# Attention scores of two heads in the two halves of the array's rows, in three passes of 64 rows

## The chip, the cores and the metric

The kernel runs on one core of one Trainium2 chip. The metric is the device time of one execution in microseconds; three runs of the kernel before took 1248.9, 1249.17 and 1249.78 us, median 1249.17. The core has a matrix engine (PE, with the loading of its weights shown apart as PEld), a vector engine (DVE), a scalar engine (ACT), a third elementwise engine (POOL) and SP, whose queue issues nearly all transfers.

## What is computed

Two layers over 512 tokens of width 1024, all in float32: an attention with a forget gate in the first, a gated short convolution in the second, each followed by an MLP with a squared ReLU and a gated embedding, with RMSNorm around everything. The change touches the attention alone, 16 heads of 64:

```python
proj = h @ w_in
q, k, v = ...                        # per head, HEAD_DIM = 64
q = q * HEAD_DIM ** -0.5
c = cumsum(log_sigmoid(f_logit))     # per head, along the tokens
s = einsum('bhqd,bhkd->bhqk', qb, k) # 128 queries at a time
s = s + cb[..., :, None] - c[..., None, :]
s = where(k_pos <= q_pos, s, NEG_INF)
pr = softmax(s)
o = einsum('bhqk,bhkd->bhqd', pr, v)
return o @ w_out
```

## The kernel before

**Numbers in two parts.** Matrix operands are kept as a pair of tiles, hi (the value rounded to the type that PE streams) and lo (the rest). `split` (L219) makes them: a copy on ACT (L221) gives hi, a subtraction on DVE (L222) gives lo. A product takes three matmuls, `mm3` (L211): hi times hi (L213), and the two mixed ones (L214, L215); the product of the two lo parts is left out. Tiles are pages of 128 x 512 from one pool of 70; matmuls write into eight PSUM banks of the same shape.

**One list for PE.** From L611 on a loop over steps `c` deals out the attention's work, and PE runs it in the order that the scheduler makes of it. `stream` (L548) supplies the filling work: `project(i)` for pair after pair of heads (48 matmuls of 512 columns each: k first, then q), then parts of the output projection (`out_part`). `share` (L614) says how many units of it are due by step `c`: two a step until the seven projections that are left are out, then 18 output units over the remaining steps. A step also has:

- `turn(h, j)` (L484): for head `h` and a block `j` of 128 keys, up to four transposes (L487) of the weights into a bank `pT`, split into `ph` and `pl`. Where columns have to be filled with zeros, POOL does it (L494).
- `mix(h, j)` (L498), two steps later (`LAG`): the values times `ph` and `pl` (L509, L510) into `ps_o`; after the last block ACT and DVE add the two halves of its rows (L514, L515).
- `scores(h, b)` (L463), eight steps ahead of the transposes: for head `h` and its block `b` of 128 queries, two matmuls (L471, L472) over `max(128 * (b + 1), 256)` key columns. Then a reduction with the bias on DVE (L474), the exponential on ACT (L478), a reciprocal on DVE (L479) and the normalisation on POOL (L480).
- `bias(h)` (L445), one head ahead of the scores (`LEAD`): four loads of the cumulated gate from DRAM on SP's queue (L457) and four masks on POOL (L458), into the tiles that the scores then become.

**How a head's score takes two matmuls.** `project(i)` brings the q of two heads into one bank, head 0 in rows 0 to 63, head 1 in rows 64 to 127, and k the same. Per head (L430 to L442) it makes three pages. `qs` holds the hi part of the head's q in the head's own 64 rows (L434, ACT) and its lo part in the other 64 rows (L435, DVE). `kh` and `kl` hold the split of k in the head's own rows, and two transfers on SP's queue (L442) copy each into the other 64 rows. A matmul over all 128 rows then adds up q-hi and q-lo times the same part of k, so that two of them, with `kh` and with `kl`, give all four products.

The last two steps' matmuls are put in order by hand (`BY_HAND`). After the loop the rest of the output projection follows (`mixer_out`, L317), and the MLP.

Of the kernel before, what the change touches and what calls it, by code (L numbers as in the profile page):

```python
# [8 lines left out]
F32 = mybir.dt.float32  # L9
F32R = mybir.dt.float32r  # L10
AF = mybir.ActivationFunctionType
ALU = mybir.AluOpType
# [3 lines left out]
P = 128  # L16
D = 1024
S = 512
H = 16
HD = 64  # L20
# [6 lines left out]
LAG = 2  # L27
# [3 lines left out]
LEAD = 1  # L31
# [4 lines left out]
BLOCKS = ((0, 0), (1, 0), (0, 1), (1, 1), (2, 1), (3, 1), (2, 0), (3, 0))  # L36
EARLY = 4
BY_HAND = 2
LEFT = 10
LATE = 0  # L40

# [21 lines left out]
def trunk(ctx: ExitStack, tc, x, pT, g, wv, wqk, bf, wo, wci, cw, wco, wup, wdn, wpp, wpg, out):  # L63
    nc = tc.nc
# [9 lines left out]
    def page(name, dtype=F32):  # L74
        return pages.tile([P, S], dtype, tag="pg", name=name)

    def bank(name):
        return psum.tile([P, S], F32, tag="ps", name=name)

    def stat(name, n=1, dtype=F32):  # L80
        return small.tile([P, n], dtype, tag=f"st{n}", name=name, bufs=32 if n == 1 else 8)
# [72 lines left out]
    def narrow(*key, k, c, soon=SOON):  # L154

        c += k % 2 * 256
        return wide(*key, k // 2, soon=soon).at(lambda u: u[:, c : c + P])
# [53 lines left out]
    def mm3(ps, a, b, start, stop):  # L211

        nc.tensor.matmul(ps, a.hi, b.hi, start=start, stop=False)  # L213
        nc.tensor.matmul(ps, a.lo, b.hi, start=False, stop=False)  # L214
        nc.tensor.matmul(ps, a.hi, b.lo, start=False, stop=stop)  # L215
        streamed[0] += 3 * ps.shape[-1]
        due()

    def split(hi, lo, src, eng=nc.vector):  # L219

        nc.scalar.copy(hi, src)  # L221
        eng.tensor_tensor(out=lo, in0=src, in1=hi.bitcast(F32), op=ALU.subtract)  # L222
# [24 lines left out]
    def stats(t, xs, name):  # L247
        return rstd([squares(xs[n][:, :S], f"{name}_q{n}_{t}") for n in range(2)], f"{name}_r{t}")
# [86 lines left out]
    def attention(hT, first_x, g0, by_hand):  # L335
# [79 lines left out]
        stacked, probs, outs, both = {}, {}, {}, {}  # L415

        def project(i):

            heads = [[page(f"{n}{i}_{e}", F32R) for n in ("qs", "kh", "kl")] for e in range(2)]
            stacked[i] = heads  # L420
            for s in (1, 0):
                ps = bank(f"qk{i}_{s}")
                for k in range(KT):
                    mm3(
                        ps, narrow("qk", i, k=k, c=s * P),
                        hT.at(lambda h: h[:, k, :]), k == 0, k == KT - 1,
                    )
                    if k < KT - 1:
                        yield
                for e in range(2):  # L430
                    a, b = slice(64 * e, 64 * e + 64), slice(64 - 64 * e, 128 - 64 * e)
                    q, kh, kl = heads[e]
                    if s == 0:
                        nc.scalar.mul(q[a, :S], ps[a, :], HD**-0.5)  # L434
                        nc.vector.scalar_tensor_tensor(  # L435
                            out=q[b, :S], in0=ps[a, :], scalar=HD**-0.5,
                            in1=q[a, :S].bitcast(F32), op0=ALU.mult, op1=ALU.subtract,
                        )
                    else:
                        split(kh[a, :S], kl[a, :S], ps[a, :])  # L440
                        for h in (kh, kl):
                            nc.sync.dma_start(h[b, :S].bitcast(F32), h[a, :S].bitcast(F32))  # L442
                yield

        def bias(h):  # L445


            i, e = h // 2, h % 2
            if e == 0:
                both[i] = page(f"pr{i}")  # L450
            long, rest = page(f"prl{h}"), page(f"prr{h}")
            probs[h] = [
                rest[:, 384:512], both[i][:, 256 * e : 256 * e + 256], rest[:, :384], long[:, :S],
            ]
            for b, pr in enumerate(probs[h]):
                n = (b + 1) * P
                nc.sync.dma_start(pr, neg_c[b, h : h + 1, :n].partition_broadcast(P))  # L457
                nc.gpsimd.affine_select(  # L458
                    out=pr[:, b * P : n], in_=pr[:, b * P : n], compare_op=ALU.is_ge,
                    fill=NEG, base=0, pattern=[[-1, P]], channel_multiplier=1,  # L460
                )

        def scores(h, b):  # L463

            q, kh, kl = stacked[h // 2][h % 2]
            n = (b + 1) * P
            nm = max(n, 256)
            pr = probs[h][b]
            ps = bank(f"sc{h}_{b}")
            qb = q[:, b * P : n]  # L470
            nc.tensor.matmul(ps[:, :nm], qb, kh[:, :nm], start=True, stop=False)  # L471
            nc.tensor.matmul(ps[:, :nm], qb, kl[:, :nm], start=False, stop=True)  # L472
            nmx, sm, rs = (stat(f"{s}{h}_{b}") for s in ("nmx", "sm", "rs"))
            nc.vector.tensor_tensor_reduce(  # L474
                out=pr, in0=ps[:, :n], in1=pr, scale=-1.0, scalar=3e38, op0=ALU.add,
                op1=ALU.min, accum_out=nmx,
            )
            nc.scalar.activation(pr, pr, AF.Exp, bias=nmx, scale=-1.0, accum_out=sm)  # L478
            nc.vector.reciprocal(rs, sm)  # L479
            nc.gpsimd.tensor_scalar(out=pr, in0=pr, scalar1=rs, scalar2=None, op0=ALU.mult)  # L480

        weights, mixed = {}, {}

        def turn(h, j):  # L484
            ps = bank(f"pT{h}_{j}")
            for b in range(j, NB):
                nc.tensor.transpose(  # L487
                    ps[:, b * P : (b + 1) * P], probs[h][b][:, j * P : (j + 1) * P], ident
                )
            lo_q = min(j * P, S - 256)  # L490
            ph, pl = page(f"ph{h}_{j}", F32R), page(f"pl{h}_{j}", F32R)
            if lo_q < j * P:
                for z in (ph, pl):
                    nc.gpsimd.memset(z[:, lo_q : j * P].bitcast(F32), 0.0)  # L494
            split(ph[:, j * P : S], pl[:, j * P : S], ps[:, j * P :])
            weights[h, j] = (ph, pl)

        def mix(h, j):  # L498

            e = h % 2  # L500
            if j == 0:
                mixed[h] = bank(f"ps_o{h}")
                if e == 0:
                    outs[h // 2] = page(f"oT{h // 2}")
            ps_o = mixed[h]
            lo_q = min(j * P, S - 256)
            v = vs[j][h // 4][:, h % 4 * P : (h % 4 + 1) * P]
            ph, pl = weights.pop((h, j))
            nc.tensor.matmul(ps_o[:, lo_q:], v, ph[:, lo_q:S], start=j == 0, stop=False)  # L509
            nc.tensor.matmul(ps_o[:, lo_q:], v, pl[:, lo_q:S], start=False, stop=j == NB - 1)  # L510
            if j == NB - 1:
                a, b = slice(64 * e, 64 * e + 64), slice(64 - 64 * e, 128 - 64 * e)
                o2 = page(f"o2{h}")
                nc.scalar.copy(o2[a, :S], ps_o[b, :])  # L514
                nc.vector.tensor_tensor(  # L515
                    out=outs[h // 2][a, :S], in0=ps_o[a, :], in1=o2[a, :S], op=ALU.add
                )
                if e == 1:
                    complete.append(h // 2)
                    split_o()  # L520
# [27 lines left out]
        def stream():  # L548
            for i in range(1, KT):
                yield from project(i)  # L550
            yield from out_part((0,), range(6))
            yield from out_part((1,), range(6))
            prepare(where["o", 1, KT - 1] + 1)
            yield from out_part((0, 1), (6,))
# [13 lines left out]
        with tc.manual_schedule(engines={E.PE, E.DVE, E.Activation}):  # L568
            r = stats(0, first_x[0], name)
# [22 lines left out]
            out=ones[:, :S], in_=ones[:, :S], compare_op=ALU.is_ge, fill=0.0, base=0,  # L592
# [15 lines left out]
        for _ in range(8):  # L608
            next(main)
        n_sc, done = 4 * H, 8  # L610
        for c in range(-8, n_sc + LAG):  # L611
            if c == n_sc - BY_HAND:
                by_hand.enter_context(tc.manual_schedule(engines={E.PE}))
            share = 2 * (c + 9) if c < n_sc - 16 else 112 + (c - n_sc + 17) * (28 - LEFT) // (15 + LAG)  # L614
            while done < share + AHEAD:
                next(main, None)
                done += 1
            if 0 <= c < n_sc:
                turn(c // 4, c % 4)
            if c >= LAG:  # L620
                mix((c - LAG) // 4, (c - LAG) % 4)
            if c + 8 < n_sc:
                scores((c + 8) // 4, c % 4)
            if c % 4 == 0 and 1 < (c + 8) // 4 + LEAD < H:
                bias((c + 8) // 4 + LEAD)
        for _ in main:
            pass
        return oT[0], banks_o
# [226 lines left out]
    hT = turned_x  # L855
    by_hand = ExitStack()
    lhs, opened = attention(hT, first_x, g0, by_hand)
    oT = lhs
    lhs = lambda k, t: tokens(oT, k, t)
# [97 lines left out]
```

## Time and profile before

| what | value |
|---|---|
| the profiled execution's own time | 1248.93 us |
| its span, first to last instruction | 1247.2 us |
| mean granted clock of PE | 0.998 |
| matmuls of the scores (L471, L472) | 64 + 64, from 81.2 to 216.9 us |
| transposes (L487) | 160, from 92.1 us on |
| mixes (L509, L510) | 64 + 64, from 96.4 to 231.1 us |
| copies of kh and kl (L442) | 16 + 16, 128 KB each |

The profile is of one execution. Times in it are microseconds unless marked ns. A matmul's row gives the line, the tile it writes, the tiles it reads, the rows and columns of the weights (128\*128) and the rows and columns of what streams (128x512). Matmuls overlap in a pipeline and their ends are modelled, so that a row's duration is longer than the distance to the next start. A wait row reads: who waited, for whom, us in total, times, longest.

### The profile page before, as it was taken

The page shows a single profiled execution, that of the slowest core. Times are in us where ns is not written, and L with a number is a line of the kernel's source. Part 1 is how long each engine was busy: PE and PEld are TensorE (multiplying, and loading weights), DVE is VectorE, ACT ScalarE, POOL GpSimd, SP SyncE. Part 2 cuts the span into 40 slices and gives each one's busy share as a digit, 9 for nine tenths or more (in the row PEclk, how much of TensorE's full clock was granted, in tenths as well). Part 3 has the DMA queues.
Part 4 walks back from the last instruction along what each step waited for, and adds up shares of the span by engine and source line. Part 5 has one row for each costly group of instructions (what it writes and reads, how often), then busy time and mean ns, then how long its engine had stood idle before and what let it go on. Part 6 is the DMA issues. An engine that isn't in the chain of part 4 may idle for free.

```text
span 1247.2 us, 18012 instructions
## 1 busy us (share of the span) xinstructions
PE 1221.6 (98%) x5972; PEld 1023.2 (82%) x5972; DVE 918.0 (74%) x1402; ACT 612.6 (49%) x1309; POOL 633.9 (51%) x631
## 2 busy tenths in 40 slices
PE   7999999999999999999999999999999999999997
PEld 6888887887888888888789888889788888888876
DVE  5657878676789778989877444457778898779972
ACT  5456777546544543454555223333654345535451
POOL 2016667256878777775211000017777778778210
PEclk9999999999999999999999999999999999999999
DMA  7456564532343224428224232432422442236401
GB/s 256 147 159 166 152 157 115 186 116 78 100 135 110 80 82 135 136 74 277 76 83 133 68 100 90 148 119 69 131 63 78 135 135 94 67 110 190 148 18 51
DMA packets 85789, 148.68 MB, mean 119 GB/s; under 512 B 10112, under 2 KB 17328, under 8 KB 85696
## 3 DMA queue, kind: packets, MB, share of 16 engines
q1 hardware_dynamic: 85488, 147.27, 38.2%
q8 instruction: 47, 0.77, 0.3%
q14 instruction: 46, 0.38, 0.1%
q10 hardware_dynamic: 144, 0.26, 0.1%
q0 software_dynamic: 64, 0.00, 0.0%
HBM read 136.93 MB, written 6.37 MB: 115 GB/s over the span
## 4 chain that ended last, share of the span: by engine, by line
PE 69%; DVE 13%; POOL 5%; issue 5%; ACT 4%; DMA 3%; SPq 0%; DVEq 0%; POOLq 0%; ACTq 0%
DVE wl L222 6%; PE up L214 6%; PE up L215 6%; PE up L213 6%; PE dn L214 5%; PE dn L213 5%; PE dn L215 5%; PE pg L213 2%; PE pg L214 2%; PE pg L215 2%; PE qk L214 2%; PE qk L213 2%; PE qk L215 2%; POOL s L715 2%; ACT junk L244 2%
## 5 line engine op out<-in xcount | busy, mean ns | idle before, releaser
L222 DVE TENSOR_TENSOR wl<-raw,wh 128x512 fp32r<-128x512 f32 (+1 forms) x404 | 364.7, 953 | 25.3 <-ACT wh L221 24.3
L221 ACT CAST wh<-raw 128x512 fp32r<-128x512 f32 (+1 forms) x404 | 219.7, 619 | 9.5 <-DVE xd L295 5.0
L214 PE MATMUL up<-hTh,wl 128*128 128x512 f32 (+1 forms) x576 | 210.1, 365 | 0.0
L215 PE MATMUL up<-hTl,wh 128*128 128x512 f32 (+1 forms) x576 | 209.8, 366 | 0.0
L213 PE MATMUL up<-hTh,wh 128*128 128x512 f32 (+1 forms) x576 | 209.3, 366 | 0.0
L222 POOL TENSOR_TENSOR wl<-T,wh 128x512 fp32r<-128x512 f32 x112 | 161.0, 1469 | 35.7 <-ACT wh L221 32.0
L213 PEld LDWEIGHTS up<-hTh,wh 128*128 128x128 f32 x576 | 108.6, 189 | 17.7
L214 PEld LDWEIGHTS up<-hTh,wl 128*128 128x128 f32 x576 | 108.6, 189 | 17.6
L215 PEld LDWEIGHTS up<-hTl,wh 128*128 128x128 f32 x576 | 108.3, 189 | 17.5 <-DVE hTl L222 0.2
L747 DVE TENSOR_TENSOR acc<-dn,acc 128x512 f32<-128x512 f32 x168 | 107.3, 679 | 8.5 <-PE dn L215 8.5
L130 POOL TENSOR_TENSOR T<-raw,raw 128x512 f32<-128x512 f32 x56 | 87.8, 1579 | 36.2 <-DMA raw<-in_wdn 23.7
L701 ACT ACTIVATE r<-up 128x512 f32<-128x512 f32 (+1 forms) x72 | 38.7, 546 | 122.7 <-PE up L215 114.7
L130 POOL TENSOR_TENSOR T<-raw,T 128x512 f32<-128x512 f32 x56 | 90.9, 1623 | 2.2
L687 DVE TENSOR_TENSOR q<-r 128x512 f32<-128x512 f32 (+1 forms) x72 | 68.6, 959 | 28.8 <-ACT r L701 28.6
L236 POOL TENSOR_SCALAR cor_r_v<-cos,cos 128x1 f32<-128x1 f32 x4 | 1.6, 398 | 159.1 <-ACT junk L244 159.1
L221 ACT CAST A11h<-q 128x256 fp32r<-128x256 f32 x28 | 11.4, 407 | 102.0 <-DVE q L687 102.0
L221 ACT CAST wh<-T 128x512 fp32r<-128x512 f32 x112 | 61.2, 617 | 0.0
L213 PE MATMUL pg<-wh,hTh 128*128 128x512 f32 x128 | 50.9, 397 | 3.5 <-ACT hTh L221 3.3
L754 POOL TENSOR_TENSOR acc<-acc,acc 128x512 f32<-128x512 f32 x28 | 46.9, 1706 | 10.1 <-DVE acc L747 10.1
L213 PE MATMUL qk<-hTh,wh 128*128 128x512 f32 x128 | 51.1, 399 | 0.0
L215 PE MATMUL qk<-hTl,wh 128*128 128x512 f32 x128 | 50.9, 397 | 0.0
L214 PE MATMUL pg<-wh,hTl 128*128 128x512 f32 x128 | 50.3, 393 | 0.0
(234 smaller groups left out, 3082.5 us busy)
## 6 DMA issues: line engine op xcount, KB each, us to landing
raw<-in_wup SPq DMA_DIRECT2D x128, 256.0 KB, 2.9
raw<-in_wdn SPq DMA_DIRECT2D x128, 256.0 KB, 2.9
raw<-in_wci SPq DMA_DIRECT2D x48, 256.0 KB, 3.2
raw<-in_wqk SPq DMA_DIRECT2D x32, 256.0 KB, 3.4
raw<-in_wpg SPq DMA_DIRECT2D x32, 256.0 KB, 3.5
g<-in_g SPq DMA_DIRECT2D x22, 256.0 KB, 5.9
prl<-neg_c SPq DMA_DIRECT2D x16, 256.0 KB, 6.6
raw<-in_wo SPq DMA_DIRECT2D x16, 256.0 KB, 5.1
```

The costliest lines, as they stand in the source:

```text
L130: nc.gpsimd.tensor_tensor(out=B[name, p], in0=B[a, p], in1=B[b, p], op=ALU.subtract)
L213: nc.tensor.matmul(ps, a.hi, b.hi, start=start, stop=False)
L214: nc.tensor.matmul(ps, a.lo, b.hi, start=False, stop=False)
L215: nc.tensor.matmul(ps, a.hi, b.lo, start=False, stop=stop)
L221: nc.scalar.copy(hi, src)
L222: eng.tensor_tensor(out=lo, in0=src, in1=hi.bitcast(F32), op=ALU.subtract)
L244: nc.scalar.activation(junk, src, AF.Square, scale=D**-0.5, accum_out=ss)
L687: nc.vector.tensor_tensor(out=out, in0=r, in1=r, op=ALU.mult)
L701: nc.scalar.activation(r[:, :n], ps[:, :n], AF.Relu)
L715: sums = lambda out, a, b, op: nc.gpsimd.tensor_tensor(out=out, in0=a, in1=b, op=op)
L747: nc.vector.tensor_tensor(out=a, in0=banks[s], in1=a, op=ALU.add)
L754: nc.gpsimd.tensor_tensor(out=a, in0=a, in1=acc[i, s][:, :S], op=ALU.add)
```

## The change

The pages of a pair are now four: `qh`, `ql`, `kh`, `kl`, each with head 0 in rows 0 to 63 and head 1 in rows 64 to 127, as the bank has them. Each is made by one instruction over 128 rows; there is no copy between rows. `scores(i, b)` takes a pair of heads: three products for each head (hi hi, hi lo, lo hi, without lo lo), each a matmul over the head's 64 rows, written in turns for head 0 and head 1 into two banks. The vector work after it is as before, head after head.

The loop is fitted to pairs: scores are issued at every second step, 12 steps ahead of the transposes instead of 8 (`SCORED`), so that the loop starts at -12; the projections run out at step 43 instead of 47, and the 18 output units are spread over the steps from 44 on; the bias of a pair's even head is issued 7 steps before its scores, that of the odd head 4 steps before.

```diff
+SCORED = 12
...
-            heads = [[page(f"{n}{i}_{e}", F32R) for n in ("qs", "kh", "kl")] for e in range(2)]
-            stacked[i] = heads
+            q, key = (Pair(page(f"{n}h{i}", F32R), page(f"{n}l{i}", F32R)) for n in "qk")
+            stacked[i] = q, key
...
-                for e in range(2):
-                    a, b = slice(64 * e, 64 * e + 64), slice(64 - 64 * e, 128 - 64 * e)
-                    q, kh, kl = heads[e]
-                    if s == 0:
-                        nc.scalar.mul(q[a, :S], ps[a, :], HD**-0.5)
-                        nc.vector.scalar_tensor_tensor(
-                            out=q[b, :S], in0=ps[a, :], scalar=HD**-0.5,
-                            in1=q[a, :S].bitcast(F32), op0=ALU.mult, op1=ALU.subtract,
-                        )
-                    else:
-                        split(kh[a, :S], kl[a, :S], ps[a, :])
-                        for h in (kh, kl):
-                            nc.sync.dma_start(h[b, :S].bitcast(F32), h[a, :S].bitcast(F32))
+                if s == 0:
+                    nc.scalar.mul(q.hi[:, :S], ps, HD**-0.5)
+                    nc.vector.scalar_tensor_tensor(
+                        out=q.lo[:, :S], in0=ps, scalar=HD**-0.5, in1=q.hi[:, :S].bitcast(F32),
+                        op0=ALU.mult, op1=ALU.subtract,
+                    )
+                else:
+                    split(key.hi[:, :S], key.lo[:, :S], ps)
...
-        def scores(h, b):
-            q, kh, kl = stacked[h // 2][h % 2]
+        def scores(i, b):
+            q, key = stacked[i]
             n = (b + 1) * P
             nm = max(n, 256)
-            pr = probs[h][b]
-            ps = bank(f"sc{h}_{b}")
-            qb = q[:, b * P : n]
-            nc.tensor.matmul(ps[:, :nm], qb, kh[:, :nm], start=True, stop=False)
-            nc.tensor.matmul(ps[:, :nm], qb, kl[:, :nm], start=False, stop=True)
...
+            heads = [(2 * i + e, slice(64 * e, 64 * e + 64), bank(f"sc{2 * i + e}_{b}")) for e in range(2)]
+            for s, (at, to) in enumerate(((q.hi, key.hi), (q.hi, key.lo), (q.lo, key.hi))):
+                for _, r, ps in heads:
+                    nc.tensor.matmul(
+                        ps[:, :nm], at[r, b * P : n], to[r, :nm], start=s == 0, stop=s == 2
+                    )
+            for h, _, ps in heads:
+                pr = probs[h][b]
...
-        for c in range(-8, n_sc + LAG):
+        for c in range(-SCORED, n_sc + LAG):
...
-            share = 2 * (c + 9) if c < n_sc - 16 else 112 + (c - n_sc + 17) * (28 - LEFT) // (15 + LAG)
+            last = n_sc - SCORED - 8
+            share = (
+                2 * (c + SCORED + 1) if c < last
+                else 112 + (c - last + 1) * (28 - LEFT) // (SCORED + 7 + LAG)
+            )
...
-            if c + 8 < n_sc:
-                scores((c + 8) // 4, c % 4)
-            if c % 4 == 0 and 1 < (c + 8) // 4 + LEAD < H:
-                bias((c + 8) // 4 + LEAD)
+            if c % 2 == 0 and c + SCORED < n_sc:
+                scores((c + SCORED) // 8, (c + SCORED) % 8 // 2)
+            for h in range(2, H):
+                if c == 8 * (h // 2) - SCORED - (7 if h % 2 == 0 else 4):
+                    bias(h)
```

More of the change, by code (lines that the diff above doesn't have):

```diff
@@ L461, in bias @@
                 )
-        def scores(h, b):
-            q, kh, kl = stacked[h // 2][h % 2]
+        def scores(i, b):
+            q, key = stacked[i]
             n = (b + 1) * P
             nm = max(n, 256)
-            pr = probs[h][b]
-            ps = bank(f"sc{h}_{b}")
-            qb = q[:, b * P : n]
[L471 to L480, printed above, removed]
+            heads = [(2 * i + e, slice(64 * e, 64 * e + 64), bank(f"sc{2 * i + e}_{b}")) for e in range(2)]
[6 more added lines that the diff above has]
+                pr = probs[h][b]
+                nmx, sm, rs = (stat(f"{s}{h}_{b}") for s in ("nmx", "sm", "rs"))
+                nc.vector.tensor_tensor_reduce(
+                    out=pr, in0=ps[:, :n], in1=pr, scale=-1.0, scalar=3e38, op0=ALU.add,
+                    op1=ALU.min, accum_out=nmx,
+                )
+                nc.scalar.activation(pr, pr, AF.Exp, bias=nmx, scale=-1.0, accum_out=sm)
+                nc.vector.reciprocal(rs, sm)
+                nc.gpsimd.tensor_scalar(out=pr, in0=pr, scalar1=rs, scalar2=None, op0=ALU.mult)
         weights, mixed = {}, {}
@@ L610, in attention @@
         n_sc, done = 4 * H, 8
-        for c in range(-8, n_sc + LAG):
+        for c in range(-SCORED, n_sc + LAG):
             if c == n_sc - BY_HAND:
                 by_hand.enter_context(tc.manual_schedule(engines={E.PE}))
-            share = 2 * (c + 9) if c < n_sc - 16 else 112 + (c - n_sc + 17) * (28 - LEFT) // (15 + LAG)
+            last = n_sc - SCORED - 8
+            share = (
+                2 * (c + SCORED + 1) if c < last
+                else 112 + (c - last + 1) * (28 - LEFT) // (SCORED + 7 + LAG)
+            )
             while done < share + AHEAD:
```

## The prediction

> **What bounds the kernel now.** I read the page's busy shares first, then the stretch from the first score to the last mix as windows, then what TensorE waits for there, then its timeline. The busy shares:
>
> ```profile
> span 1247.2 us, 18012 instructions
> PE 1221.6 (98%) x5972; PEld 1023.2 (82%) x5972; DVE 918.0 (74%) x1402; ACT 612.6 (49%) x1309; POOL 633.9 (51%) x631
> PE 69%; DVE 13%; POOL 5%; issue 5%; ACT 4%; DMA 3%; SPq 0%; DVEq 0%; POOLq 0%; ACTq 0%
> ```
>
> TensorE leaves 25.6 us of the span idle, and it is 69% of the chain that ended last. The first score matmul starts at 81.46 us and the last mix at about 231; in windows over that stretch (window, length, then busy time of PE, PEld, DVE, ACT, POOL, granted clock, DMA share, GB/s):
>
> ```profile
> 110.00:140.00 30.00, 29.36 (x159) 25.02 (x158) 24.37 (x67) 21.19 (x54) 19.81 (x33) 1.00 0.57 166
> 170.00:200.00 30.00, 29.24 (x161) 25.04 (x160) 25.74 (x72) 23.05 (x59) 22.20 (x32) 1.00 0.61 155
> 200.00:232.00 32.00, 30.74 (x168) 25.25 (x167) 22.55 (x64) 21.65 (x55) 19.07 (x30) 1.00 0.32 78
> sum 150.54, PE 147.88 PEld 125.25 DVE 117.55 ACT 109.48 POOL 98.87; mean PE 29.58 PEld 25.05 DVE 23.51 ACT 21.90 POOL 19.77
> ```
>
> PE is idle for 150.54 - 147.88 = 2.66 us of the whole stretch, at full clock. The waits of PE, from 65 to 240 us, name nearly all of it:
>
> ```profile
> PE ps_o L509 <- POOL ph L494: 1.4, 2, 0.8
> PE ps_o L509 <- DVE pl L222: 0.8, 1, 0.8
> PE pT L487 <- DVE pl L222: 0.4, 1, 0.4
> ```
>
> No wait is for a score operand or for a copy between rows. So the stage is as long as PE's own list of matmuls, and the change has to be priced there, matmul by matmul.
>
> **Prices on PE.** A matmul's listed duration contains a pipeline that the next one overlaps; the price is the distance between starts.
>
> ```profile
> 81.46 0.28 PE L471 MATMUL sc<-kh,qs 128*128 128x256 f32 x1
> 81.57 0.28 PE L472 MATMUL sc<-kl,qs 128*128 128x256 f32 x1
> 81.69 0.28 PE L471 MATMUL sc<-kh,qs 128*128 128x256 f32 x1
> 81.81 0.28 PE L472 MATMUL sc<-kl,qs 128*128 128x256 f32 x1
> 81.93 0.34 PE L471 MATMUL sc<-kh,qs 128*128 128x384 f32 x1
> 82.11 0.34 PE L472 MATMUL sc<-kl,qs 128*128 128x384 f32 x1
> 82.28 0.39 PE L213 MATMUL qk<-hTh,wh 128*128 128x512 f32 x1
> ...
> 83.67 0.39 PE L471 MATMUL sc<-kh,qs 128*128 128x512 f32 x1
> 83.90 0.40 PE L472 MATMUL sc<-kl,qs 128*128 128x512 f32 x1
> 84.13 0.39 PE L213 MATMUL qk<-hTh,wh 128*128 128x512 f32 x1
> ```
>
> Four matmuls of 256 columns take 81.46 to 81.93, 0.1175 us each; 384 columns 0.175; 512 columns 0.23. One head (two passes over 256, 256, 384, 512) costs 2 x 0.64 = 1.28 us, sixteen heads **20.5 us**. That is what the change replaces.
>
> **The matmuls after.** Each pair of heads now has six matmuls a block, three per head, of the same column counts but 64 rows. If one streams after the other, as every matmul in this trace does, that is 8 pairs x 6 x 0.64 = **30.7 us, +10.2**. Rows buy nothing in the one place where fewer than 128 go in (a single row, in another number format, so a far row):
>
> ```profile
> L853 PE MATMUL g<-row,one 1*128 1x512 f32 x4 | 3.7, 1088 | 6.4 <-DMA row<-in_g 6.4
> L370 PE MATMUL ps_c<-tri,lf_h 128*16 128x512 f32 x1 | 0.4, 397 | 0.0
> ```
>
> Nor does a sixteenth of the columns of weights: 397 ns, as for a full one. Time goes by columns streamed. The other end is that two heads, sitting in different halves of the rows, stream at the same time. No row shows such a pair. But the order in which the changed program issues to PE limits even this: its 192 score matmuls stand in 45 unbroken runs, and 23 of these, with 55 matmuls worth 9.9 us, hold one head alone (three of one head, a mix or a projection, three of the other). Walking the other 22 runs, each matmul starting beside its partner and after its own head's previous one, gives 11.6 us. So side by side the list is 9.9 + 11.6 = **21.5 us, still +1.0**: three passes paired where they can be are no cheaper than two full ones. The bounds of this term are +1.0 and +10.2. I take +10.2, since the nearest rows show streams following each other.
>
> The Trainium skill, page "TensorE: Matmul & The Clock Gate", section "Part 3: Packing small matmuls — row/col tiling", says matmuls in distinct row groups run concurrently, and gives 3.07x for four groups of 32 rows and 512 columns. No run here shows it; by it the term would be the +1.0.
>
> **Weights.** Each matmul loads its 128 columns of weights, and a load shows its own limit where the stream is short:
>
> ```profile
> 111.36 0.27 PE L487 MATMUL pT<-ident,prr 128*128 128x128 f32 x1
> 111.47 0.27 PE L487 MATMUL pT<-ident,pr 128*128 128x128 f32 x1
> ...
> 47.96 0.22 PE L370 MATMUL ps_c<-tri,lf_h 128*16 128x128 f32 x1
> 48.01 0.22 PE L370 MATMUL ps_c<-tri,lf_l 128*16 128x128 f32 x1
> ```
>
> With 128 columns of weights 128 streamed columns cost 0.11, with 16 columns 0.05: the load takes 0.11. One after another, loads stay covered (0.1175 and more). Side by side they would not if two halves cannot load together: starts 0.11 apart in the same walk give **26.6 us, +6.1**.
>
> **Changing between full and half array.** 45 runs are 90 changes. The trace has none that isn't followed by a wait, so 0 is one bound. The nearest price is a matmul whose weights could not be loaded ahead:
>
> ```profile
> 227.00 0.50 PE L509 MATMUL ps_o<-ph,v 128*128 128x512 f32 x1 [0.83 <-DVE pl L222]
> 227.33 0.39 PE L510 MATMUL ps_o<-pl,v 128*128 128x512 f32 x1
> 227.56 0.39 PE L213 MATMUL o<-wh,hTh 128*128 128x512 f32 x1
> ```
>
> 0.33 instead of 0.23, 0.10 more; 90 x 0.10 = 9.0 us. Above that stands a full emptying of the pipeline: duration less distance, 0.39 - 0.23 = 0.16, or 14.4 us. For streams that follow each other I take 0, because nothing in this trace ties a change of rows to a stall.
>
> **What leaves the other engines.** For each pair two heads' splits become one:
>
> ```profile
> L434 ACT ACTIVATE qs<-qk x16: 590/592/595, 76.2 to 202.5; 64x512 fp32r<-64x512 f32 x16
> L435 DVE SCALAR_TENSOR_TENSOR qs<-qk,qs x16: 683/688/694, 76.8 to 203.1; 64x512 fp32r<-64x512 f32 x16
> L221 ACT CAST kh<-qk x16: 563/580/584, 70.8 to 194.8; 64x512 fp32r<-64x512 f32 x16
> L442 SPq DMA_DIRECT2D kh<-kh x16: 461/467/957, 71.4 to 195.5; - x16
> L222 DVE TENSOR_TENSOR kl<-qk,kh x16: 674/688/697, 71.4 to 196.4; 64x512 fp32r<-64x512 f32 x16
> ```
>
> Half of the 32 ACT and of the 32 DVE instructions go, since a 128-row one has the same columns: ACT loses 8 x (0.592 + 0.580) = 9.4 us, DVE 16 x 0.688 = 11.0. SP loses 32 issues of about 0.47 (the kl copies priced as the kh ones), 15 us of its queue. All of it lies under PE; DVE at its fullest is 25.74 of 30. It can shorten only the two waits on DVE above (1.2 us); the larger wait is for POOL's memset of ph, whose queue loses nothing.
>
> **What moves.** Scores are issued 12 steps ahead instead of 8, and projections run out at step 43 instead of 47; a step is about 150.5/74 = 2.0 us. A pair's bias (per head four loads of neg_c on SP and four masks on POOL) goes with its scores: the even head's 7 steps earlier, 7 before its first use instead of 4, the odd head's 8 earlier, still 4 before. On POOL a mask that waits for its load holds up the normalisations behind it, and those hold the transposes. Four steps are 8 us, and a load lands in 6.6:
>
> ```profile
> prl<-neg_c SPq DMA_DIRECT2D x16, 256.0 KB, 6.6
> ```
>
> So no lead becomes shorter, and SP reaches the loads sooner for the copies it no longer issues. At the end the scores are out by step 50 instead of 55, and the same 18 output units are spread over 22 steps instead of 18: fewer fillers between the last transposes and mixes, whose stall now is the 0.83 above; one or two more such are +0.8 to +1.7. The bounds of everything beside the list: -2.7 (no PE idle left) to +1.7. I take 0.
>
> **Sum.** The profiled execution took 1248.93 us, span 1247.2 and 1.73 around it. 1248.93 + 10.2 = 1259.1. The median of the runs, 1249.17, is 0.24 higher: **1259.4**.
>
> **Rivals**, on the median.
> - *Side by side, nothing else* (the other side): 1249.2 + 1.0, less at most 2.7: 1247.5 to 1250.2. For it: the heads sit in separate rows and banks, and most runs alternate heads. Against: no row shows overlapped streams. Within 0.2% (2.5 us, about what a measurement of this kernel can tell from no change) in nearly all of its range; to be faster it must also win time that the trace doesn't list as idle, such as loads that are not covered.
> - *Side by side, loads in turn*: +6.1, 1255.3. For it: every load in the timeline starts only when the matmul before it starts.
> - *Side by side, but every change between full and half array costs*: +1.0 and 9.0 to 14.4, 1259.2 to 1264.6. For it: the order really interleaves scores with projections and transposes, 90 changes; against: no such stall in this trace. The Trainium skill, "TensorEngine Tiling (Array Packing)", section "Tiling Modes", has this rule: changing the mode, not just the tile, drains the TensorE. No run here shows it.
> - *One after another, and every change costs*: +10.2 and 9.0 to 14.4, 1268 to 1274.
>
> That the copies stay cannot be: the changed program issues none.
>
> **Chances.** Forecast 0.30; side by side with costly changes 0.27; loads in turn 0.14; both costs 0.10; side by side alone 0.19, of which 0.12 within 0.2% and 0.07 faster. So slower 0.81. The range leaves out the last case's fast part and the one with both costs, 0.17: 1247 to 1268. The forecast's own range is 10.2 with -2.7 to +1.7: 1256.7 to 1261.1.
>
> **What would show it.** Right: 192 score matmuls whose starts within a run are 0.12, 0.175 and 0.23 apart, the first matmul after a run no later than its columns, and every line after 240 us shifted by some 10 us. Side by side: starts of a pair nearly together. Loads in turn: 0.11 apart whatever the columns. Costly changes: the gap before the first and after the last of a run is 0.1 or more wider. The forecast is wrong if PE's waits in the stretch grow well beyond 2.66 us, or if the pairs start together.

## The result and the profile after

The changed kernel takes 1263.6 us (median of four runs, 1262.86 to 1263.86) beside 1249.47 for the kernel before on the same chip: a ratio of 1.0109, 95% interval 1.0092 to 1.0127, or +14.1 us. The profiled execution took 1263.86 us. From the page of the changed kernel, the span, the busy shares, and the chain's shares by engine:

```profile
span 1262.1 us, 18000 instructions
PE 1238.7 (98%) x6036; PEld 1022.3 (81%) x6036; DVE 906.1 (72%) x1386; ACT 604.0 (48%) x1293; POOL 627.5 (50%) x631
PE 60%; DVE 18%; POOL 7%; issue 6%; ACT 6%; DMA 3%; SPq 1%; DVEq 0%; POOLq 0%; ACTq 0%
```

The span grew by 14.9 us, and PE's busy time by 17.1. The windows over the attention's stretch in the changed kernel (window, length, busy time of PE, PEld, DVE, ACT, POOL, granted clock, DMA share, GB/s), and PE's waits from 65 to 255 us:

```profile
112.00:142.00 30.00, 30.00 (x161) 22.66 (x162) 19.82 (x60) 18.04 (x48) 15.07 (x26) 1.00 0.37 107
202.00:247.00 45.00, 44.23 (x231) 33.44 (x230) 31.68 (x83) 28.53 (x72) 20.81 (x35) 1.00 0.18 59
sum 165.00, PE 164.23 PEld 122.51 DVE 108.39 ACT 101.82 POOL 92.02; mean PE 32.85 PEld 24.50 DVE 21.68 ACT 20.36 POOL 18.40
```

```profile
PE ps_o L509 <- DVE pl L223: 0.7, 2, 0.5
```

The stretch that ended at about 231 us now ends at about 247, at full clock, with PE idle for 0.77 us of it instead of 2.66. The other engines do have less to do (DVE 108.39 us in 165 instead of 117.55 in 150.54). So the added time is neither a wait nor a slower clock: it is in PE's own list. The timeline shows where. First a run of twelve score matmuls, then one of six, each between projections (start, duration, engine, line, operation, tiles, weights, stream; x2 are two matmuls put together in one row):

```profile
81.71 0.39 PE L216 MATMUL qk<-hTl,wh 128*128 128x512 f32 x1
82.03 0.38 PE L468 MATMUL sc<-kh,qh 64*128 64x256 f32 x2
82.25 0.28 PE L468 MATMUL sc<-kl,qh 64*128 64x256 f32 x2
82.37 0.28 PE L468 MATMUL sc<-kh,ql 64*128 64x256 f32 x2
82.49 0.29 PE L468 MATMUL sc<-kh,qh 64*128 64x256 f32 x2
82.60 0.29 PE L468 MATMUL sc<-kl,qh 64*128 64x256 f32 x2
82.72 0.29 PE L468 MATMUL sc<-kh,ql 64*128 64x256 f32 x2
82.94 0.50 PE L214 MATMUL qk<-hTh,wh 128*128 128x512 f32 x1
83.28 0.40 PE L215 MATMUL qk<-hTh,wl 128*128 128x512 f32 x1
...
89.22 0.39 PE L216 MATMUL qk<-hTl,wh 128*128 128x512 f32 x1
89.54 0.50 PE L468 MATMUL sc<-kh,qh 64*128 64x512 f32 x2
89.88 0.40 PE L468 MATMUL sc<-kl,qh 64*128 64x512 f32 x2
90.11 0.39 PE L468 MATMUL sc<-kh,ql 64*128 64x512 f32 x2
90.44 0.50 PE L214 MATMUL qk<-hTh,wh 128*128 128x512 f32 x1
90.77 0.40 PE L215 MATMUL qk<-hTh,wl 128*128 128x512 f32 x1
```

Two things are to be seen. The two heads stream side by side: a row of two matmuls of 256 columns is followed by the next after 0.12 us (82.25, 82.37, 82.49), the price of one full matmul; two of 512 columns take 0.23 (89.88 to 90.11). In the trace's starts, the partners of the first pair are 3 ns apart. And each run (the score matmuls that PE takes one behind the other, with no other matmul between them) has four gaps of about 0.1 us beyond the prices of its matmuls. After the projection at 89.22 the first pair starts at 89.54 instead of 89.45 (0.09). The second pair comes 0.34 after the first instead of 0.23 (0.11). The projection after the last pair starts 0.33 later instead of 0.23 (0.10), and the one behind it again 0.33 (0.10). Together that is 0.40 us by these rounded starts; **0.41 us a run**, 0.20 a change, is the figure used below. A change is a passage from full to half array or back, so a run has two. The run of twelve has the same four gaps and no more. The weight loads of the changed kernel, in the same view, point to what two of the four are:

```profile
89.54 0.19 PEld L468 LDWEIGHTS sc<-kh,qh 64*128 64x128 f32 x2 [0.35 <-issue]
89.65 0.19 PEld L468 LDWEIGHTS sc<-kl,qh 64*128 64x128 f32 x2
89.88 0.19 PEld L468 LDWEIGHTS sc<-kh,ql 64*128 64x128 f32 x2
90.43 0.19 PEld L214 LDWEIGHTS qk<-hTh,wh 128*128 128x128 f32 x1 [0.37 <-DVE nmx L474]
90.54 0.19 PEld L215 LDWEIGHTS qk<-hTh,wl 128*128 128x128 f32 x1
```

At a change the first load starts with its own matmul (89.54, 90.43), and the next load comes only 0.11 after it, while the first matmul is listed with 0.50 us instead of 0.39. I read this as a first load that could not be made ahead: the first matmul's row contains it, and the second matmul is late by it. Within a run, the loads of both halves start together (x2). Loads do not go in turn.

### The profile page after: what moved, and what is told of

The parts are those of the page before. It is cut to its first block, busy times and chain, and to the rows that moved or that the text cites. A ratio compares the mean times of both kernels' runs of the same rounds, so it can differ in the third digit from the quotient of the medians.

```text
span 1262.1 us, 18000 instructions
## 1 busy us (share of the span) xinstructions
PE 1238.7 (98%) x6036; PEld 1022.3 (81%) x6036; DVE 906.1 (72%) x1386; ACT 604.0 (48%) x1293; POOL 627.5 (50%) x631
## 4 chain that ended last, share of the span: by engine, by line
PE 60%; DVE 18%; POOL 7%; issue 6%; ACT 6%; DMA 3%; SPq 1%; DVEq 0%; POOLq 0%; ACTq 0%
DVE wl L223 10%; POOL s L720 4%; PE up L215 3%; PE up L216 3%; PE up L214 3%; ACT wh L222 3%; PE dn L215 3%; PE qk L214 3%; PE dn L216 3%; PE dn L214 3%; DVE acc L752 2%; PE qk L216 2%; PE qk L215 2%; PE sc L468 2%; PE pg L214 2%
## 5 line engine op out<-in xcount | busy, mean ns | idle before, releaser
L222 ACT CAST A11h<-q 128x256 fp32r<-128x256 f32 x28 | 11.4, 407 | 99.9 <-DVE q L692 99.9
L216 PE MATMUL qk<-hTl,wh 128*128 128x512 f32 x128 | 50.8, 397 | 0.0
L215 PE MATMUL qk<-hTh,wl 128*128 128x512 f32 x128 | 50.5, 395 | 0.0
```

## The experiments

To compare kernels, I sum the distances between the starts of all matmuls, from the last one before the first score to the second behind the last mix. Scores: over all runs, from the time when a run's first matmul would be due to the start of the second matmul behind the run, less the price of the first one behind it; waits within that time count too. Other gaps: everything else above the prices by distance, waits and stretches at a lower clock alike. The rest of the list is 124.0 us with the loop of before and 123.3 with the new one.

| kernel | runs of scores | scores | other gaps | stretch |
|---|---|---|---|---|
| before | 63 | 24.4 | 1.9 | 150.3 |
| changed | 45 | 38.4 | 3.6 | 165.3 |
| loop_full | 51 | 26.9 | 8.9 | 159.0 |
| loop_full_dve | 49 | 23.7 | 4.2 | 151.2 |
| before_dve | 66 | 24.1 | 0.8 | 148.9 |
| before_hand | 62 | 22.2 | 11.5 | 157.8 |
| hand_order | 31 | 28.1 | 4.9 | 156.3 |
| hand_two_blocks | 16 | 23.0 | 10.9 | 157.2 |
| two_blocks_tuned | 16 | 27.9 | 7.2 | 158.4 |
| apart | 62 | 54.8 | 2.4 | 180.5 |
| dummy_half | 72 | 50.8 | 0.3 | 175.1 |
| dummy_full | 69 | 31.1 | 0.3 | 155.4 |
| refill_splits | 31 | 29.3 | 11.4 | 164.0 |
| refill_hand | 31 | 30.1 | 25.5 | 178.9 |

Each row is one profiled execution. Those of before_hand (1257.54 us), refill_hand (1277.45) and refill_splits (1263.64) were 1.6 to 3 us longer than the medians given below.

The theory: heads stream side by side (the list costs +1.0), and each run of half-array matmuls costs 0.41 us. The rivals: the cost comes with matmuls of 64 rows as such, or from the new loop, or from moved work on other engines.

**loop_full: the new loop with the old operands.** Everything of the change stays but the pages and the matmuls, which are those of before, copies included.

```diff
...
-            heads = [... bank(f"sc{2 * i + e}_{b}")) for e in range(2)]
-            for s, (at, to) in enumerate(((q.hi, key.hi), (q.hi, key.lo), (q.lo, key.hi))):
-                ...
+            for e, (_, _, ps) in enumerate(heads):
+                q, kh, kl = stacked[i][e]
+                qb = q[:, b * P : n]
+                nc.tensor.matmul(ps[:, :nm], qb, kh[:, :nm], start=True, stop=False)
+                nc.tensor.matmul(ps[:, :nm], qb, kl[:, :nm], start=False, stop=True)
```

> The changed loop (pairs, 12 steps ahead, the new bias steps) with the operands and the two full-array matmuls of before, copies included. Theory A (each run of half-array matmuls costs about 0.41 us beside its streams: 0.09 before its first, 0.10 in its second pass, 0.10 at its end, 0.11 behind it): nothing of the loss is left, 1247 to 1252. Theory B (the loss is the third pass, streams one after another): the same, as there is no third pass. Theory C (the loss is the new loop: bank pairs, bias steps, fewer fillers at the end): 1258 to 1264.

Measured: 1258.08 us, ratio 1.0065 (1.0050 to 1.0080). The loop alone costs 8.1 us, with no half-array matmul in the kernel. That is what the rival "the new loop" forecast, and not what the theory did; the later runs have to say why the changed kernel's own trace shows so little of it (other gaps 3.6, here 8.9). PE's waits from 65 to 255 us, then POOL's timeline before the longest of them and PE's at its end, all of loop_full (the bracket: idle time before, and what ended it):

```profile
PE ps_o L513 <- POOL ph L498: 7.2, 5, 1.9
```

```profile
181.44 0.29 POOL L459 TENSOR_SCALAR_AFFINE_SELECT pr<-pr 128x128 f32<-128x128 f32 x1 [1.81 <-DMA pr<-neg_c]
183.41 0.29 POOL L459 TENSOR_SCALAR_AFFINE_SELECT prr<-prr 128x128 f32<-128x128 f32 x1 [1.68 <-DMA prr<-neg_c]
185.25 0.29 POOL L459 TENSOR_SCALAR_AFFINE_SELECT prl<-prl 128x128 f32<-128x128 f32 x1 [1.54 <-DMA prl<-neg_c]
185.93 0.29 POOL L459 TENSOR_SCALAR_AFFINE_SELECT pr<-pr 128x128 f32<-128x128 f32 x1 [0.39 <-DMA pr<-neg_c]
186.17 0.20 POOL L498 MEMSET ph<- 128x128 f32 x1
```

```profile
186.43 0.62 PE L513 MATMUL ps_o<-ph,v 128*128 128x256 f32 x2 [1.94 <-POOL ph L498]
```

Four masks stand ahead of the zeroing of `ph` in POOL's queue, and each waits for its bias load. The zeroing waits behind them, and the mix waits for the zeroing.

**before_hand and hand_order: PE in the written order.** In the kernel before and in the changed one, PE takes its list in the order of the program's text from the loop's first step on (-8 in the kernel before), not only in the last two steps.

```diff
-            if c == n_sc - BY_HAND:
+            if c == -SCORED:
                 by_hand.enter_context(tc.manual_schedule(engines={E.PE}))
```

> The kernel before with PE's order taken from the program text through the whole loop, instead of the scheduler's. It is the control for the next two: what the written order costs by itself. All theories: 0 to +8 us, through waits on PE that the scheduler had filled, none of them at a score.

> The changed kernel with PE's order taken from the program text: its 192 score matmuls then stand in 31 runs instead of 45, all pairs whole, and nothing is computed otherwise. Theory A: the scores take 15.4 us side by side and 31 x 0.41 = 12.7, 28.1 instead of 40.2 in the trace of the changed kernel; so 12 us less than it, 1251 to 1252, plus what the written order costs by itself. Theory B: streams and columns are the same, so no less than 1263. Theory C: the loop is the same, 1263.

Measured: before_hand 1254.59 us, ratio 1.0041 (1.0026 to 1.0057); hand_order 1254.7, ratio 1.0041 (1.0026 to 1.0056), 8.9 less than the changed kernel (12 less were expected, before the price of the written order itself, which before_hand puts at 4.7). In the changed kernel, the written order brings 45 runs down to 31, all of them of both heads: by the walk of the prediction 15.4 us side by side, plus 31 x 0.41 = 12.7, is 28.1; the starts sum to 28.1. PE's largest waits from 65 to 255 us, first of before_hand, then of hand_order:

```profile
PE ps_o L509 <- POOL ph L494: 4.2, 6, 0.7
```

```profile
PE o L216 <- DVE wl L223: 0.9, 2, 0.5
```

In the same written order the two kernels take the same time, but not for the same reason: the paired scores cost 5.9 more on PE (28.1 against 22.2), and the other gaps are 6.6 less (4.9 against 11.5; part of this is that before_hand's profiled execution was a long one).

**hand_two_blocks: half as many runs.** The scores of a pair are issued for two blocks at once, every fourth step, in the written order; the first two blocks share a bank.

```diff
...
-            if c % 2 == 0 and c + SCORED < n_sc:
-                scores((c + SCORED) // 8, (c + SCORED) % 8 // 2)
+            if c % 4 == 0 and c + SCORED < n_sc:
+                scores((c + SCORED) // 8, (0, 1) if (c + SCORED) % 8 == 0 else (2, 3))
```

> The last one with the scores of two blocks issued together at every fourth step (the first two blocks of a head share a bank): 16 runs of 12. Theory A: 15.4 + 16 x 0.41 = 22.0 us, 6 us less than with 31 runs, 1245 to 1247 plus what the written order and the scarcer banks cost. Theory B and C: as with 31 runs, or more through the banks.

Measured: 1255.28 us, ratio 1.0042 (1.0026 to 1.0059). The scores fall to 23.0 us (15.4 + 16 x 0.41 = 22.0 was to be expected), but the time doesn't: the other gaps grow from 4.9 to 10.9. What the runs gave back is lost to waits, the longest for POOL's zeroing of `ph` (2.1 us), and to a granted clock of 0.94 from 110 to 140 us, an estimated 30 x 0.06 = 1.8 us at most.

**apart: the same matmuls, one head at a time.** As hand_order, but each step issues one head's three matmuls instead of two heads' six at every second step.

```diff
-            heads = [(2 * i + e, slice(64 * e, 64 * e + 64), bank(f"sc{2 * i + e}_{b}")) for e in range(2)]
+            heads = [(2 * i + e, slice(64 * e, 64 * e + 64), bank(f"sc{2 * i + e}_{b}"))]
...
-            if c % 2 == 0 and c + SCORED < n_sc:
-                scores((c + SCORED) // 8, (c + SCORED) % 8 // 2)
+            if c + SCORED < n_sc:
+                scores((c + SCORED) // 8, (c + SCORED) % 8 // 2, c % 2)
```

> The written order of hand_order, but head 1's three matmuls of a block are issued one step after head 0's: the same matmuls in 62 runs of one head each. Theory A (about 0.41 us for each run, and heads in different halves stream at the same time only when they stand together): no pairs, 30.7 us of streams, and 62 x 0.41 = 25.4; 56.1 instead of 28.1, so 28 us more than hand_order, 1281 to 1284. Theory B (64-row matmuls stream one after another anyway; runs cost nothing): as hand_order, 1255. Theory C: as hand_order.

Measured: 1279.12 us, ratio 1.0234 (1.0214 to 1.0255), 24.4 more than hand_order and a little under the expectation. The scores rise by 26.7 us, of which 15.3 is the lost pairing (30.7 against 15.4) and the other 11.4 belongs to 31 more runs, 0.37 each. One such run in apart's timeline of PE:

```profile
95.02 0.40 PE L216 MATMUL qk<-hTl,wh 128*128 128x512 f32 x1
95.35 0.38 PE L468 MATMUL sc<-kh,qh 64*128 64x256 f32 x1
95.57 0.28 PE L468 MATMUL sc<-kl,qh 64*128 64x256 f32 x1
95.69 0.27 PE L468 MATMUL sc<-kh,ql 64*128 64x256 f32 x1
95.89 0.50 PE L214 MATMUL qk<-hTh,wh 128*128 128x512 f32 x1
```

Three matmuls of one head, 256 columns each, take 0.54 us (95.35 to 95.89), as long as hand_order's six of two heads (0.55 by the starts), and have the same gaps.

**dummy_half and dummy_full: a change and nothing else.** In the kernel before, each score gets a third matmul of 128 columns ahead of its two, whose result the next one overwrites. In dummy_half it has 64 rows, in dummy_full 128; nothing else differs.

```diff
+            nc.tensor.matmul(ps[:, :P], q[:64, b * P : n], kh[:64, :P], start=True, stop=True)
             nc.tensor.matmul(ps[:, :nm], qb, kh[:, :nm], start=True, stop=False)
             nc.tensor.matmul(ps[:, :nm], qb, kl[:, :nm], start=False, stop=True)
```

> The kernel before with one more matmul in front of each head's two score matmuls: 64 rows, 128 columns, into the bank that the next one overwrites; 64 in all, standing alone between full-array ones. Theory A: each is a run of its own, 0.41 and its 0.05 of columns, 64 x 0.46 = 29 us: 1277 to 1281. Theory B: columns and a load of weights alone, 64 x 0.11 = 7 us, 1256.

> The control: the same 64 extra matmuls over all 128 rows. Every theory: the price of a load of weights, 64 x 0.11 = 7 us, 1255 to 1258.

Measured: dummy_half 1273.31 us, ratio 1.0188 (1.0168 to 1.0208); dummy_full 1253.13, ratio 1.0025 (1.0014 to 1.0035). The same 64 matmuls cost 20.2 us more with 64 rows than with 128. Both came out lower than expected; 1.6 us of that is in the other gaps, 1.9 in the kernel before and 0.3 in both variants. PE's timeline around one such matmul, in dummy_half and in dummy_full:

```profile
95.88 0.27 PE L488 MATMUL pT<-ident,prl 128*128 128x128 f32 x1
96.08 0.32 PE L471 MATMUL sc<-kh,qs 64*128 64x128 f32 x1
96.34 0.50 PE L215 MATMUL qk<-hTl,wh 128*128 128x512 f32 x1
96.67 0.40 PE L213 MATMUL qk<-hTh,wh 128*128 128x512 f32 x1
```

```profile
97.47 0.22 PE L471 MATMUL sc<-kh,qs 128*128 128x128 f32 x1
97.53 0.39 PE L472 MATMUL sc<-kh,qs 128*128 128x384 f32 x1
```

With 64 rows, it starts 0.20 behind a transpose instead of 0.11, the matmul behind it 0.26 later, and the one behind that 0.33 later instead of 0.23. With 128 rows, the next starts 0.06 later. Over all 64 the difference is 0.32 us each and not 0.41, since the 128-row matmul has a price too: by the table the scores with it take (31.1 - 24.4) / 64 = 0.10 us more each. So a run of one pays for the change too, and the cost has nothing to do with pairs, with the new loop or with q and k in their new pages.

**two_blocks_tuned: an attempt at a faster version.** As hand_two_blocks, with mixes three steps behind the transposes, weights of the output projection prepared three tiles ahead instead of one, and the zeroing on DVE.

```diff
-LAG = 2
+LAG = 3
...
-O_SOON = 1
+O_SOON = 3
...
-                    nc.gpsimd.memset(z[:, lo_q : j * P].bitcast(F32), 0.0)
+                    nc.vector.memset(z[:, lo_q : j * P].bitcast(F32), 0.0)
```

> hand_two_blocks (16 runs) with what its trace showed waiting taken away: mixes three steps after their transposes instead of two, the zeroing of ph and pl on DVE instead of POOL, the weights of the output projection split three tiles ahead instead of one. Theory A: scores stay at 23.0 us against 24.4 in the kernel before; if the 10.9 us of other waits shrink to the 1.9 that the kernel before has, 1247; if they stay, 1255. Theory B and C give no gain from 16 runs.

Measured: 1255.8 us, ratio 1.0048 (1.0031 to 1.0064): no gain on hand_two_blocks. The waits for POOL are gone, others have come (the scores with their waits 27.9 instead of 23.0). The granted clock was lower too, 0.94 from 170 to 200 us, 0.91 from 200 to 225 and 0.95 from 225 to 250, which is worth an estimated 5.3 us at most; without it the time would be about that of the kernel before. So neither version with sixteen runs wins, but that sixteen can't is not shown.

**refill_hand and refill_splits: the removed work put back beside the new matmuls.** As hand_order, with the splits of a pair made a second time into pages that nothing reads; refill_hand also issues the copies between rows, refill_splits does not. One thing is not as it was: the second split of q goes into the pages that the copies wrote, and ACT waited for a copy there once, 2.9 us.

```diff
...
+                mirror = [page(f"m{s}{n}{i}", F32R) for n in "hl"] if s else mirror
+                split(mirror[0][:, :S], mirror[1][:, :S], ps)
+                if s:
+                    for e in range(2):
+                        a, b = slice(64 * e, 64 * e + 64), slice(64 - 64 * e, 128 - 64 * e)
+                        for m, h in zip(mirror, (key.hi, key.lo)):
+                            nc.sync.dma_start(m[b, :S].bitcast(F32), h[a, :S].bitcast(F32))
```

> hand_order with the work that the change took off the other engines put back into pages that nobody reads: per pair two more ACT and two more DVE instructions of 512 columns and four copies between rows of 128 KB each; PE's list stays the same. If that work lies beside PE, as I costed it: 0 to +1.2 us, 1255 to 1256. If it set the end anywhere: up to the 11 us that DVE spends on it, 1266.

> refill_hand (1275.8) without its 32 copies: only the 16 + 16 extra ACT and DVE instructions are put back into hand_order (1254.7). If the 21 us came from the copies, which stand before the bias loads on SP's queue and share the transfer engines with them, so that POOL's masks and the zeroing behind them come late: 1255 to 1257. If they came from DVE and ACT, or from the projections' banks being held longer: 1270 or more.

Measured: refill_hand 1275.84 us, ratio 1.0199 (1.0181 to 1.0218), 21 more than hand_order; refill_splits 1261.54, ratio 1.0082 (1.0066 to 1.0099), 6.8 more. Both expectations missed: I had put the removed work at 0 to 1.2 us, and then the return of the splits at nothing or at all of the 21. By the times, a third of it comes with the splits and two thirds with the copies, in this order of PE; both traces also have stretches at a lower clock (last section), so that these shares are rough. PE's largest wait in refill_hand, then POOL's largest:

```profile
PE ps_o L517 <- POOL ph L502: 8.0, 3, 3.4
```

```profile
POOL prr L462 <- DMA prr<-neg_c: 32.5, 18, 3.1
```

The same wait in hand_order:

```profile
POOL prr L454 <- DMA prr<-neg_c: 19.8, 15, 2.3
```

The copies stand on SP's queue before the bias loads; the masks wait for these, the zeroing waits behind the masks, and the mixes wait for the zeroing, as in loop_full.

**loop_full_dve and before_dve: the zeroing taken out of POOL's queue.** In loop_full and in the kernel before, one line moves to DVE.

```diff
-                    nc.gpsimd.memset(z[:, lo_q : j * P].bitcast(F32), 0.0)
+                    nc.vector.memset(z[:, lo_q : j * P].bitcast(F32), 0.0)
```

> loop_full, whose PE waited 7.2 us for POOL's zeroing of ph, with that zeroing on DVE. If the loop's +8 us are POOL's queue (the zeroing stands behind normalisations and masks): 1250 to 1252. If the loop costs by its order or its banks: 1258.

> The kernel before with the same one edit, the zeroing on DVE. Its PE waits 1.4 us for it: 1248 to 1249.5, a gain that is hardly above what can be told, or none if the next wait takes its place.

Measured: loop_full_dve 1249.69 us, ratio 0.9994 (0.9985 to 1.0003); before_dve 1247.79, ratio 0.9977 (0.9968 to 0.9986). One moved line takes 8.4 us off loop_full. The fair comparison is between these two, which differ by the loop alone: 1.9 us are left of its 8.1. So most of what the loop cost came through the zeroing in POOL's queue. PE's largest waits from 65 to 255 us, in loop_full_dve and in before_dve:

```profile
PE pT L491 <- POOL prl L484: 2.2, 1, 2.2
```

```profile
PE ps_o L509 <- DVE pl L222: 1.2, 1, 1.2
```

No mix waits for `ph` any more. before_dve is the fastest of all, but by little: 2.8 us (0.23%) under the kernel before on the same chip, and 15.8 under the changed one's median.

## Why the prediction came out as it did

The direction, the place and the range were right: slower, all of it in the stretch from the first score to the last mix (+15.0 of the span's +14.9), on PE's own list, with fewer waits than before. But the mechanism that I held likeliest was not the one, and its own range, 1256.7 to 1261.1, was missed: that the forecast +10.2 lies near the measured +14.1 is luck. The time is that of the rival "side by side, but every change between full and half array costs" (1259.2 to 1264.6; measured 1263.6).

**The step that failed first** is "+10.2, since the nearest rows show streams following each other". A row of before can't show what two heads in different halves do, since none had two. The partners of the first pair start 3 ns apart, and the walk over the issue order was right: 21.5 us for the list, +1.0. The Trainium skill, page "TensorE: Matmul & The Clock Gate", section "Part 3: Packing small matmuls — row/col tiling", says that matmuls in distinct row groups run concurrently, and the trace agrees: two matmuls of 512 columns in 0.23 us. The rival "loads in turn" falls by the load rows above.

**The step that failed second** is "I take 0, because nothing in this trace ties a change of rows to a stall". By the sums, scores with their gaps took 38.4 us; less the list of 21.5 that is 16.9 over 90 changes, **0.19 a change** (less than 0.20, in part since nine pairs of runs have a single matmul between them and share a gap). dummy_half shows the price by itself. The bounds were off too: 0.10 and 0.16 were an uncovered load and an emptied pipeline as alternatives, and a change has gaps of both kinds, about 0.10 ahead of the first matmul and 0.10 between first and second. That the first gap is the emptying is read from the starts; no run separated the two. The Trainium skill, page "TensorEngine Tiling (Array Packing)", section "Tiling Modes", has it that a change of mode drains TensorE; the trace agrees that the change has a price, 0.41 us for going and coming back, and does not show that it is a drain.

The sum as it was: list +1.0, changes +16.9, gaps that the 63 runs of before had around their scores -3.9 (24.4 less 20.5 of columns), other gaps +1.7, the rest of the list -0.7: +15.0, as measured for the stretch. The rival's term for the changes, 9.0 to 14.4, was too small for the 16.9; the 3.9 had no term in the prediction. That the time fell into the rival's range all the same is luck too: the one error made up for the other.

**What leaves the other engines** was right in that no time came back: PE's idle time fell from 2.66 to 0.77 us, but the other gaps, which also count delays that the listed durations hide, grew by 1.7. **What moves**, taken as 0 with at most +1.7, was right in its sum and wrong as a step: with the old operands the same loop costs 8.1, most of it through POOL's queue, which the prediction named and then let go. In the changed kernel this does not appear. Likely two things hide it: with neither copies nor second splits the masks are ready sooner (putting both back in the written order cost 21 us, the splits alone 6.8), and a longer list on PE leaves them more time (in dummy_half and dummy_full the other gaps fall from 1.9 to 0.3, in apart from hand_order's 4.9 to 2.4). What each is worth under the scheduler's order was not tried.

One reading was wrong and nothing hangs on it: 16 columns of weights are an eighth of 128, not a sixteenth.

**Why the pairing did not pay here.** In whole pairs it saves 20.5 - 15.4 = 5.1 us of list, and it also does away with the gaps that the old scores had: against the 24.4 us of the scores before, 9.0 us are to be had, against before_hand's 22.2 in the written order, 6.8. At 0.41 a run these are used up by 22 and by 17 runs. The change has 45. Two blocks at a time have 16, which is just at the limit: 23.0 us, 1.4 less than before and 0.8 more than before_hand. Eight runs, one for each pair of heads, would take an estimated 15.4 + 8 x 0.41 = 18.7 us, but hold six of the eight banks at once; that wasn't tried.

## What to carry to other kernels

In this kernel half-array matmuls could pay only in long unbroken runs. Count, in the order in which PE really gets its list, how often it goes from full to half array and back, and set the price of each such excursion, 0.41 us here, against what the pairing saves. A price that no row of the trace shows is not 0 for that: a rival that rests on it deserves the weight that its mechanism has in the issue order. And before moving work between steps, read the queues that run in order: in loop_full a zeroing of 0.2 us, behind masks that wait for loads, held PE up for 7.2 us.

## What the runs showed of the hardware

The heads overlap even where the program issues one after the other. In the order issued, the last run has head 0's three matmuls ahead of head 1's three, yet the changed kernel's timeline has them in pairs:

```profile
226.82 0.71 PE L468 MATMUL sc<-kh,qh 64*128 64x512 f32 x2
227.16 0.61 PE L468 MATMUL sc<-kl,qh 64*128 64x512 f32 x2
227.39 0.61 PE L468 MATMUL sc<-kh,ql 64*128 64x512 f32 x2
227.93 0.44 PE L510 MATMUL ps_o<-pl,v 128*128 128x384 f32 x1
```

The second head's first matmul, fourth in the program, starts second, 0.22 us behind the first head's; the six take 1.11 us instead of the 1.59 that one after another would be at these prices with the same gaps (6 x 0.23 + 0.11 + 0.10). Five other runs, of 256 columns, are issued as two of head 0, two of head 1, then one of each, and take 0.55 us, as long as those issued in turns.

And where PE had waited long, its granted clock was lower. A window of refill_hand, then one of refill_splits, columns as above:

```profile
200.00:230.00 30.00, 28.20 (x141) 20.99 (x142) 21.05 (x55) 18.78 (x46) 14.14 (x27) 0.90 0.51 105
```

```profile
200.00:230.00 30.00, 27.59 (x144) 20.41 (x143) 21.46 (x64) 19.45 (x52) 17.00 (x27) 0.89 0.16 49
```

The clock is 0.90 to 0.94 in all of refill_hand's windows from 110 to 230 us, and 1.00 throughout in hand_order's. One such place in hand_two_blocks shows what it does: behind a wait of PE of 2.12 us that ends at 114.39, the granted clock is 0.50 from 115.0 to 118.2, and projections of 512 columns start 0.43 apart (115.08, 115.51, 115.94) instead of 0.23, and from 118.41 on 0.23 again. By the windows the clock may make up to 30 x (0.06 + 0.06 + 0.07 + 0.10) = 8.7 us of refill_hand's 21, and up to 3.3 of refill_splits's 6.8, by estimate. A wait alone does not settle it: loop_full waited up to 1.94 us at a time and kept its clock at 1.00. What decides it stays open.
